# Weight slots of 1024 columns at set distances from the activations, and the first stage's K tiles in two units

## The chip, the cores and the metric

The kernel runs on one core of one Trainium2 chip. The metric is the device time of one execution in microseconds. The kernel before takes 1234.42 us, the median of three runs (1234.06 to 1234.61).

## What is computed

One layer of a hybrid decoder for 256 tokens and a model width of 2048, in float32. Cut to its products:

```
h    = rmsnorm(x) ; proj = h @ w_in          # pool group | q | k | v | indexer q, k, weights
pool = trailing means minus token, per-group linear map, scale
attn = attention of 8 heads over the 64 keys per query that the indexer picks, with a T5 bias
x   += concat(pool, attn) @ w_out
u    = rmsnorm(x) @ w_up                     # 2048 x 11264
uc   = causal depthwise conv of width 3 of u
x   += (silu(gate) * val) @ w_down           # 5632 x 2048
x   += (p @ w_ple_proj) * sigmoid(rmsnorm(x) @ w_ple_gate)
out  = rmsnorm(x)
```

## The kernel before, in words

Every weight passes through SBUF once, in units. `unit` (lines 59 to 68) loads n columns with a DMA on SP's queue into a tile `raw`, has ScalarE (ACT) copy them to `hi` in the type float32r, which drops low bits, and VectorE (DVE) write `lo = raw - hi`, so that hi + lo is exact. There are four slots for raw, three for hi and three for lo; each slot is UNIT = 1104 columns wide, which is what the first stage needs (one K tile of 128 rows of v, indexer keys and head weights is 1104 columns). Slots are taken in turn, and a slot is taken again when what reads it is done. All other stages load units of 1024 columns. The activations are kept as hi and lo parts side by side, 256 columns each.

The products come in two forms. In `cm_matmul` (line 121) the weights are stationary: for each of the eight K tiles of a unit, TensorE (PE) loads a 128x128 tile of hi and streams hT's 512 columns (activations' hi and lo), then loads the tile of lo and streams 256 columns. `cm_tile` (line 130) makes one column tile of 128 outputs of two units: 32 such tiles in the mixer (indexer queries, q and k, the pool group), 88 in the up-projection. In `tm_matmul` (line 143) the activations are stationary and 512 columns of the unit are streamed, three times for each K tile and half of the tokens: 12 matmuls a unit. So are the first stage (368 columns, 16 K tiles, lines 210 to 230), the output projection (32 units, activations `catP` and `catA`), the down-projection (88 units, `aT`) and the gate (32 units, `hT`; the last 8 are kept in tiles of their own).

A load of the next stationary tile goes on while the matmul before it streams. Each engine runs its instructions in order. The order is made by a planner when the program is built, from its own model of times; `keep_in_program_order` pins some of the DMAs. SP's queue carries nearly all loads. ACT's queue carries a few: among them the table of relative biases is written to DRAM (`bd`, line 326) and read back shifted (`tb`, line 328), and the second waits for the first.

Tiles are laid out in SBUF one pool behind the other, in the order in which the pools are opened. In the built program of before a partition holds, by byte address: hT 36064; raw 74240, 78656, 83072, 87488; hi 91904, 96320, 100736; lo 105152, 109568, 113984; then small buffers, catP 125952, and in the later stages aT 132096. The three pairs of hi and lo slots are called A, B and C in the order of their addresses. A tile of hT has 2048 bytes, a K tile of a unit 512 bytes where the weights are stationary and 2048 where they stream. Modulo 512, hi and lo lie this far beyond hT: A 32 and 480, B 352 and 288, C 160 and 96; aT lies beyond hi and lo: A 256 and 320, B 448 and 0, C 128 and 192.

Of the kernel before, what the change touches and what calls it, by code (L numbers as in the profile page):

```python
# [10 lines left out]
F32 = mybir.dt.float32  # L11
# [7 lines left out]
P = 128  # L19
# [9 lines left out]
TOPK = 64  # L29
# [4 lines left out]
NVK = (NH * P + 80) // 3  # L34
UNIT = 3 * NVK

# columns of the packed per-channel parameters
C_GMIX, C_GFFN, C_GPLE, C_PS, C_CONV = 0, 16, 32, 48, 56
# columns of the packed constants
K_ACC0, K_ACC1, K_PEN0, K_PEN1, K_OH, K_INV = 0, 128, 384, 512, 768, 1152  # L40
# [4 lines left out]
def layer(ctx: ExitStack, tc: tile.TileContext, a: dict):  # L45
    nc = tc.nc
    in_order = tc.keep_in_program_order
    V, A, T, G = nc.vector, nc.scalar, nc.tensor, nc.gpsimd

    cst = ctx.enter_context(tc.tile_pool(name="cst", bufs=1))  # L50
    wraw = ctx.enter_context(tc.tile_pool(name="wraw", bufs=4))
    whi = ctx.enter_context(tc.tile_pool(name="whi", bufs=3))
    wlo = ctx.enter_context(tc.tile_pool(name="wlo", bufs=3))
    tmp = ctx.enter_context(tc.tile_pool(name="tmp", bufs=2))
# [4 lines left out]
    def unit(src, n=1024, keep=None):  # L59
        """n weight columns on chip as the exact sum hi + lo of two float32r parts"""  # L60
        size, bufs = (1024, 8) if keep else (UNIT, None)
        raw = wraw.tile([P, UNIT], F32, name="raw")
        nc.sync.dma_start(raw[:, :n], src)
        hi = (keep or whi).tile([P, size], F32R, name="hi", bufs=bufs)
        A.copy(hi[:, :n], raw[:, :n])  # L65
        lo = (keep or wlo).tile([P, size], F32R, name="lo", bufs=bufs)
        V.tensor_sub(lo[:, :n], raw[:, :n], hi[:, :n].bitcast(F32))  # L67
        return hi, lo

# [1 line left out]
    prm = cst.tile([P, C_CONV + S], F32, name="prm")  # L71
# [49 lines left out]
    def cm_matmul(ps, hi, lo, kts, first, last):  # L121
        """weights stationary: ps[:, :256] + ps[:, 256:] = w.T @ hT"""
        for i, kt in enumerate(kts):
            w = slice(i * P, (i + 1) * P)
            T.matmul(ps, hi[:, w], hT[:, kt, :], start=first and i == 0, stop=False)  # L125
            T.matmul(ps[:, :S], lo[:, w], hT[:, kt, :S],  # L126
                     start=False, stop=last and i == len(kts) - 1)
# [15 lines left out]
    def tm_matmul(pss, hi, lo, act, kts, first, last, toks=(0, 1), n=512, w0=0):  # L143
        """activations stationary: pss[t] = act[:, tok t].T @ w"""
        for i, kt in enumerate(kts):
            w = slice(w0 + i * n, w0 + (i + 1) * n)
            for t in toks:
                xh = act[:, kt, t * P:(t + 1) * P]
                xl = act[:, kt, S + t * P:S + (t + 1) * P]
                T.matmul(pss[t][:, :n], xh, hi[:, w], start=first and i == 0, stop=False)  # L150
                T.matmul(pss[t][:, :n], xh, lo[:, w], start=False, stop=False)  # L151
                T.matmul(pss[t][:, :n], xl, hi[:, w], start=False,  # L152
                         stop=last and i == len(kts) - 1)

    def to_hT(n, gcol):
        """columns n*512.. of the residual stream, transposed, times g, split"""
        for kp in range(2):
            ps = aux.tile([P, 512], F32, name="ps")
            for j in range(2):
                kt = 4 * n + 2 * kp + j  # L160
                for t in range(2):
                    T.transpose(ps[:, j * S + t * P:j * S + (t + 1) * P],  # L162
                                x[:, t, kt * P:(kt + 1) * P], ident)
            for j in range(2):
                kt = 4 * n + 2 * kp + j
                split(hT[:, kt, :S], hT[:, kt, S:], ps[:, j * S:(j + 1) * S],
                      prm[:, gcol + kt:gcol + kt + 1])
# [15 lines left out]

    # =====================================================================
    with ExitStack() as c1:
        ar = c1.enter_context(tc.tile_pool(name="ar", bufs=1))
        catP = ar.tile([P, 8, 2 * S], F32R, name="catP")

# [1 line left out]
        xr = [ar.tile([P, 8, S], F32, name="xr0", tag="tb"),  # L190
# [10 lines left out]

        # the tensor engine's clock rises while the first loads are under way
        warm = aux.tile([P, 512], F32, name="ps")
# [4 lines left out]
        for kt in range(KT):  # L208
            if kt == 1 or (kt and kt % 2 == 0):
                k1 = kt + 1 if kt == 1 else kt + 2  # L210
                nc.sync.dma_start(xr[kt // 8][:, kt % 8:(k1 - 1) % 8 + 1, :],
                                  a["xT"][:, kt:k1, :])
            cuts = (0, NVK, 3 * NVK) if kt == 0 else (0, 3 * NVK)
            ws = [unit(a["w_first"][kt][:, c0:c1], c1 - c0) for c0, c1 in zip(cuts, cuts[1:])]
            split(hT[:, kt, :S], hT[:, kt, S:],
                  xr[kt // 8][:, kt % 8, :] if kt else prm[:, C_CONV:],
                  prm[:, C_GMIX + kt:C_GMIX + kt + 1])
            for n in range(3):
                i = sum(n * NVK >= c for c in cuts) - 1
                tm_matmul(pvk[n], *ws[i], hT, (kt,), kt == 0, kt == KT - 1, n=NVK,  # L220
                          w0=n * NVK - cuts[i])
            if kt == 3:
                in_order(nc.sync.dma_start(ident, a["ident"]))
            if kt in (5, 7, 9, 11):
                c = (kt - 5) // 2
                cs = slice(c * 512, (c + 1) * 512)
                in_order(nc.sync.dma_start(x[:, :, cs], a["x"][:, :, cs]))
            if kt in (9, 11, 13, 15):
                square_x((kt - 9) // 2)
# [5 lines left out]

# [1 line left out]
        kd = ar.tile([P, 2, 2, 64], F32, name="kd")  # L237
# [25 lines left out]

# [1 line left out]
        s0 = [cc[:, K_ACC0:K_ACC0 + P], cc[:, K_ACC1:K_ACC1 + S]]  # L265
        sc = [ar.tile([P, P], F32, name="sc0"), ar.tile([P, S], F32, name="sc1")]

        def query(ps):
            """fp32 for the first 128 tokens; for the others the rows of a head are followed
            by (or follow) their low parts, so that one product over 128 rows takes both"""  # L270
            qx = ar.tile([P, S], F32, name="qx", bufs=3)
# [47 lines left out]

# [1 line left out]
        psb = aux.tile([P, 512], F32, name="ps")  # L321
# [8 lines left out]

# [1 line left out]
        one = ar.tile([P, S], F32, name="one")  # L332
# [29 lines left out]

# [1 line left out]
        L = [ar.tile([P, NH, P], F32, name="L0"), ar.tile([P, NH, S], F32, name="L1", tag="L1")]  # L364
# [67 lines left out]

# [1 line left out]
        plr = None  # L434
# [56 lines left out]

# [1 line left out]
        def out_units(n, pss, gs, first, last):  # L493
# [17 lines left out]

    # =====================================================================
    pin = ctx.enter_context(tc.tile_pool(name="pin", bufs=1))
# [4 lines left out]
    with ExitStack() as c2:  # L518
        far = c2.enter_context(tc.tile_pool(name="far", bufs=1))
        aT = far.tile([P, NF, 2 * S], F32R, name="aT")  # L520
        r_ffn = rstd_col(sum4(ssq_f), "r_ffn")
# [22 lines left out]

        # the first two tiles leave the last K tiles to the end: those come from the last
        # columns of the residual stream
        ps2 = [acc.tile([P, 512], F32, name="pa") for _ in range(2)]
# [7 lines left out]

# [1 line left out]
        for n in range(4):  # L557
# [6 lines left out]

    # =====================================================================
    with ExitStack() as c3:
# [27 lines left out]
        def store(t, slots):  # L594
            """the last slot joins the sum of those before it"""
            ms = gar.tile([P, 1], F32, name=f"ms{t}")
# [44 lines left out]
def _cm(w):  # L641
    """(K, C) -> (C/128, 128, K/128*128): rows of a partition for one column tile together"""
    k, c = w.shape
    return np.ascontiguousarray(
        w.reshape(k // P, P, c // P, P).transpose(2, 1, 0, 3).reshape(c // P, P, k))


def _tm(w, n=512):
    """(K, N) -> (N/512, 128, K/128*512)"""
    k, c = w.shape  # L650
    return np.ascontiguousarray(
        w.reshape(k // P, P, c // n, n).transpose(2, 1, 0, 3).reshape(c // n, P, k // P * n))
# [72 lines left out]
```

## Time and profile before

| | |
|---|---|
| median of the runs | 1234.42 us |
| span of the profiled execution | 1232.6 us; the runs lie 1.5 to 2.0 us above it |
| PE busy | 1199.4 us, 97% of the span, 6332 matmuls |
| PE weight loads busy | 1027.0 us, 83% |
| DVE, ACT busy | 816.1 us (66%), 625.5 us (51%) |
| PE, up-projection's hi and lo matmuls with the mixer's | 1904 of each |
| DMA | 230.44 MB, mean 187 GB/s; 352 GB/s in the first of 40 slices |
| granted clock | 0.989 of 2.4 GHz, mean over the span |

PE's busy time counts each matmul from its start to a modelled end, and matmuls overlap, so the sum of durations is more than the time they take. The distance between the starts of two matmuls in a row is what one costs. Times in the timeline are us from the span's start.

### The profile page before, as it was taken

How to read it: one execution, taken by the hardware profiler on the slowest of the kernel's cores; microseconds unless marked ns; L12 is line 12 of the kernel's file. 1: busy time of each engine (PE TensorE's matmuls, PEld its weight loads, DVE VectorE, ACT ScalarE, POOL GpSimd, SP SyncE). 2: the span in 40 equal slices, each digit the busy share in tenths (PEclk: the TensorE clock that was granted, in tenths of full speed). 3: DMA queues.
4: the chain of work that ended last, by engine and by line, in shares of the span. 5: the costliest groups of instructions: out<-in, count | busy, mean ns of one | idle time of the engine just before them, and what ended most of it. 6: DMA issues, size and time to landing. Idle time of an engine off the chain costs nothing.

```text
span 1232.6 us, 16720 instructions
## 1 busy us (share of the span) xinstructions
PE 1199.4 (97%) x6332; PEld 1027.0 (83%) x6332; DVE 816.1 (66%) x1234; ACT 625.5 (51%) x951; POOL 5.5 (0%) x23
## 2 busy tenths in 40 slices
PE   9999669999999999999999999999999999999996
PEld 8988558888888888888888888888888888888886
DVE  6566465796555877787777877788645454545565
ACT  7455134565454655555555555555434343434453
POOL 0000000000000000000000000000000000000000
PEclk9999879999999999999999999999999999999998
DMA  9654555545655655555555565566666666666662
GB/s 352 222 185 146 126 171 191 161 148 178 188 173 168 210 190 189 189 188 189 189 189 190 189 190 190 191 189 192 189 188 185 190 182 191 181 194 213 188 217 87
DMA packets 67784, 230.44 MB, mean 187 GB/s; under 512 B 7416, under 2 KB 11128, under 8 KB 67576
## 3 DMA queue, kind: packets, MB, share of 16 engines
q1 hardware_dynamic: 63488, 223.88, 57.8%
q10 hardware_dynamic: 4216, 5.51, 2.1%
q8 instruction: 49, 0.80, 0.3%
q14 instruction: 31, 0.25, 0.1%
HBM read 225.16 MB, written 3.67 MB: 186 GB/s over the span
## 4 chain that ended last, share of the span: by engine, by line
PE 95%; DMA 3%; ACT 1%; DVE 0%; SPq 0%; issue 0%; POOLq 0%; ACTq 0%
PE pa L125 35%; PE pa L126 18%; PE pa L151 12%; PE pa L152 12%; PE pa L150 12%; DMA bd<-bv 3%; PE ps L151 1%; PE ps L152 1%; PE ps L150 1%; PE ps L162 1%; DMA raw<-in_w_first 0%; PE ps L465 0%; PE ps L290 0%; ACT hi L65 0%; PE ps L375 0%; PE ps L291 0%
## 5 line engine op out<-in xcount | busy, mean ns | idle before, releaser
L67 DVE TENSOR_TENSOR lo<-raw,hi 128x1024 fp32r<-128x1024 f32 (+2 forms) x417 | 508.5, 1220 | 373.5 <-ACT hi L65 370.6
L65 ACT CAST hi<-raw 128x1024 fp32r<-128x1024 f32 (+2 forms) x417 | 435.8, 1046 | 555.3 <-issue 218.7
L125 PE MATMUL pa<-hT,hi 128*128 128x512 f32 x1904 | 667.8, 394 | 20.3 <-ACT hi L65 20.3
L126 PE MATMUL pa<-hT,lo 128*128 128x256 f32 x1904 | 534.5, 281 | 0.5 <-DVE lo L67 0.5
L125 PEld LDWEIGHTS pa<-hT,hi 128*128 128x128 f32 x1904 | 358.4, 188 | 102.4 <-ACT hi L65 21.0
L126 PEld LDWEIGHTS pa<-hT,lo 128*128 128x128 f32 x1904 | 358.6, 188 | 1.2 <-DVE lo L67 1.0
L152 PE MATMUL pa<-hi,aT 128*128 128x512 f32 x352 | 138.4, 393 | 0.0
L151 PE MATMUL pa<-lo,aT 128*128 128x512 f32 x352 | 138.3, 393 | 0.0
L150 PE MATMUL pa<-hi,aT 128*128 128x512 f32 x352 | 125.9, 395 | 0.0
L151 PEld LDWEIGHTS pa<-lo,aT 128*128 128x128 f32 x352 | 66.0, 188 | 15.6
L152 PEld LDWEIGHTS pa<-hi,aT 128*128 128x128 f32 x352 | 66.0, 188 | 15.1
L150 PEld LDWEIGHTS pa<-hi,aT 128*128 128x128 f32 x352 | 66.1, 188 | 15.0
L151 PE MATMUL pa<-lo,hT 128*128 128x512 f32 (+2 forms) x208 | 74.4, 358 | 0.1
L152 PE MATMUL pa<-hi,hT 128*128 128x512 f32 (+2 forms) x208 | 74.3, 358 | 0.0
L150 PE MATMUL pa<-hi,hT 128*128 128x512 f32 (+2 forms) x208 | 64.4, 359 | 1.4 <-ACT hi L65 1.4
L532 ACT ACTIVATE cv<-ub,cnv 128x256 f32<-128x256 f32 x88 | 52.6, 598 | 1.0 <-DVE ub L141 1.0
L140 DVE TENSOR_TENSOR eb<-pa,eb 128x256 f32<-128x256 f32 x119 | 49.6, 417 | 0.0
L536 DVE SCALAR_TENSOR_TENSOR cv<-ub,cnv,cv 128x256 f32<-128x256 f32 x88 | 42.6, 485 | 3.0
L150 PEld LDWEIGHTS pa<-hi,hT 128*128 128x128 f32 x208 | 38.3, 188 | 7.2 <-ACT hi L65 2.0
L151 PEld LDWEIGHTS pa<-lo,hT 128*128 128x128 f32 x208 | 39.1, 188 | 5.7 <-DVE lo L67 0.7
L139 ACT COPY eb<-pa 128x256 f32<-128x256 f32 x119 | 43.5, 365 | 0.0
L152 PEld LDWEIGHTS pa<-hi,hT 128*128 128x128 f32 x208 | 39.1, 188 | 5.0
(171 smaller groups left out, 822.2 us busy)
## 6 DMA issues: line engine op xcount, KB each, us to landing
raw<-in_w_up SPq DMA_DIRECT2D x176, 512.0 KB, 3.8
raw<-in_w_down SPq DMA_DIRECT2D x88, 512.0 KB, 3.6
raw<-in_w_qk SPq DMA_DIRECT2D x32, 512.0 KB, 3.9
raw<-in_w_out SPq DMA_DIRECT2D x32, 512.0 KB, 3.7
raw<-in_w_pg SPq DMA_DIRECT2D x32, 512.0 KB, 3.9
raw<-in_w_first SPq DMA_DIRECT2D x15, 552.0 KB, 6.4
raw<-in_w_qi SPq DMA_DIRECT2D x16, 512.0 KB, 4.6
raw<-in_w_u SPq DMA_DIRECT2D x16, 512.0 KB, 3.7
```

What stands on the lines that cost most here:

```text
L65: A.copy(hi[:, :n], raw[:, :n])
L67: V.tensor_sub(lo[:, :n], raw[:, :n], hi[:, :n].bitcast(F32))
L125: T.matmul(ps, hi[:, w], hT[:, kt, :], start=first and i == 0, stop=False)
L126: T.matmul(ps[:, :S], lo[:, w], hT[:, kt, :S], start=False, stop=last and i == len(kts) - 1)
L139: A.copy(b, ps[:, S:])
L140: V.tensor_add(b, ps[:, :S], b)
L150: T.matmul(pss[t][:, :n], xh, hi[:, w], start=first and i == 0, stop=False)
L151: T.matmul(pss[t][:, :n], xh, lo[:, w], start=False, stop=False)
L152: T.matmul(pss[t][:, :n], xl, hi[:, w], start=False, stop=last and i == len(kts) - 1)
L162: T.transpose(ps[:, j * S + t * P:j * S + (t + 1) * P], x[:, t, kt * P:(kt + 1) * P], ident)
L532: A.activation(t, u[:, 2:], AF.Identity, bias=cnv[:, k + 3:k + 4], scale=cnv[:, k + 2:k + 3])
L536: V.scalar_tensor_tensor(t, u[:, :S], cnv[:, k:k + 1], t, op0=OP.mult, op1=OP.add)
```

## The change

UNIT becomes 1024, so every slot has 4096 bytes, and the slots of one part (raw, hi or lo) have the same address modulo 1024. Pools with one tile each that nothing reads or writes are opened between raw and hi (16 columns of 4 bytes) and between hi and lo (240 columns), and one of 80 columns stands ahead of aT. A K tile of the first stage no longer fits a slot and is loaded, split and multiplied in two units of 736 and 368 columns (K tile 0 was two units of 368 and 736 before, and stays so). Comments are dropped from the file. The diff without them:

```
-UNIT = 3 * NVK
+UNIT = 1024
...
     wraw = ctx.enter_context(tc.tile_pool(name="wraw", bufs=4))
+    gap0 = ctx.enter_context(tc.tile_pool(name="gap0", bufs=1))
     whi = ctx.enter_context(tc.tile_pool(name="whi", bufs=3))
+    gap1 = ctx.enter_context(tc.tile_pool(name="gap1", bufs=1))
     wlo = ctx.enter_context(tc.tile_pool(name="wlo", bufs=3))
...
+    def place(pool, n):
+        pool.tile([P, n], F32, name="place")
+
+    place(gap0, 16)
+    place(gap1, 240)
...
-            cuts = (0, NVK, 3 * NVK) if kt == 0 else (0, 3 * NVK)
+            cuts = (0, NVK, 3 * NVK) if kt == 0 else (0, 2 * NVK, 3 * NVK)
...
         far = c2.enter_context(tc.tile_pool(name="far", bufs=1))
+        place(far, 80)
         aT = far.tile([P, NF, 2 * S], F32R, name="aT")
```

## Rows read from the trace of the kernel before

**Rows 1.** Busy time of each engine in stretches: from:to in us, length, then busy us and instructions of PE, weight loads, DVE, ACT, POOL, the granted clock, DMA share and GB/s.

```profile
8.50:13.30 4.80, 4.39 (x24) 3.78 (x24) 3.55 (x5) 4.40 (x6) 0.00 (x0) 1.00 1.03 404
13.30:49.50 36.20, 36.20 (x217) 36.20 (x216) 22.11 (x30) 22.93 (x40) 0.70 (x1) 1.00 0.89 325
...
400.00:888.00 488.00, 488.00 (x2789) 427.50 (x2788) 388.16 (x616) 280.04 (x438) 0.00 (x0) 1.00 0.60 191
888.00:1136.00 248.00, 248.00 (x1090) 201.40 (x1089) 119.89 (x117) 103.59 (x120) 0.69 (x1) 1.00 0.65 191
```

**Rows 2.** The page's chain of the work that ended last: shares of the span by engine, then by line.

```profile
PE 95%; DMA 3%; ACT 1%; DVE 0%; SPq 0%; issue 0%; POOLq 0%; ACTq 0%
PE pa L125 35%; PE pa L126 18%; PE pa L151 12%; PE pa L152 12%; PE pa L150 12%; DMA bd<-bv 3%; PE ps L151 1%; PE ps L152 1%; PE ps L150 1%; PE ps L162 1%; DMA raw<-in_w_first 0%; PE ps L465 0%; PE ps L290 0%; ACT hi L65 0%; PE ps L375 0%; PE ps L291 0%
```

**Rows 3.** PE's timeline in the up-projection: start in us, length in us, engine, line, tiles. The first matmul of four units in a row, in the slots B, A, C, B.

```profile
704.61 0.39 PE L125 MATMUL pa<-hT,hi 128*128 128x512 f32 x1
...
707.36 0.39 PE L125 MATMUL pa<-hT,hi 128*128 128x512 f32 x1
...
710.14 0.40 PE L125 MATMUL pa<-hT,hi 128*128 128x512 f32 x1
...
712.96 0.39 PE L125 MATMUL pa<-hT,hi 128*128 128x512 f32 x1
```

**Rows 4.** The same view early in the up-projection: hi matmuls of a unit in slot B that begins at 404.06 us, and the start of the next unit, 406.87.

```profile
404.06 0.39 PE L125 MATMUL pa<-hT,hi 128*128 128x512 f32 x1
...
404.40 0.40 PE L125 MATMUL pa<-hT,hi 128*128 128x512 f32 x1
...
404.75 0.40 PE L125 MATMUL pa<-hT,hi 128*128 128x512 f32 x1
...
405.82 0.39 PE L125 MATMUL pa<-hT,hi 128*128 128x512 f32 x1
...
406.16 0.40 PE L125 MATMUL pa<-hT,hi 128*128 128x512 f32 x1
...
406.87 0.39 PE L125 MATMUL pa<-hT,hi 128*128 128x512 f32 x1
```

**Rows 5.** The same view in the mixer, units in slot B that come first behind other work on PE: hi matmuls that are five pairs apart, in the units that begin at 95.96, 228.67 and 254.68 us.

```profile
95.96 0.39 PE L125 MATMUL pa<-hT,hi 128*128 128x512 f32 x1
...
97.73 0.39 PE L125 MATMUL pa<-hT,hi 128*128 128x512 f32 x1
...
229.82 0.39 PE L125 MATMUL pa<-hT,hi 128*128 128x512 f32 x1
...
231.58 0.39 PE L125 MATMUL pa<-hT,hi 128*128 128x512 f32 x1
...
255.93 0.39 PE L125 MATMUL pa<-hT,hi 128*128 128x512 f32 x1
...
257.69 0.39 PE L125 MATMUL pa<-hT,hi 128*128 128x512 f32 x1
```

**Rows 6.** The same view where the up-projection begins.

```profile
397.93 0.39 PE L125 MATMUL pa<-hT,hi 128*128 128x512 f32 x1
398.57 0.51 PE L125 MATMUL pa<-hT,hi 128*128 128x512 f32 x1 [0.25 <-ACT hi L65]
```

**Rows 7.** The same view in the down-projection: the first two matmuls of four units in a row, in the slots A, C, B, A.

```profile
950.07 0.63 PE L150 MATMUL pa<-hi,aT 128*128 128x512 f32 x2
...
952.85 0.62 PE L150 MATMUL pa<-hi,aT 128*128 128x512 f32 x2
...
955.60 0.63 PE L150 MATMUL pa<-hi,aT 128*128 128x512 f32 x2
...
958.40 0.63 PE L150 MATMUL pa<-hi,aT 128*128 128x512 f32 x2
```

**Rows 8.** Groups of ACT's instructions by line and shape in the first stage, 3 to 55 us: count, busy us, mean ns of one, idle us before them and what ended it.

```profile
L65 ACT CAST hi<-raw 128x1104 fp32r<-128x1104 f32 x15 | 16.7, 1116 | 12.6 <-PE ps L152 10.3 <-DMA raw<-in_w_first 1.9 <-DVE hT L94 0.2
...
L65 ACT CAST hi<-raw 128x736 fp32r<-128x736 f32 x1 | 0.8, 804 | 1.8 <-DMA raw<-in_w_first 1.8
...
L65 ACT CAST hi<-raw 128x368 fp32r<-128x368 f32 x1 | 0.5, 498 | 0.0
```

**Rows 9.** The same for DVE.

```profile
L67 DVE TENSOR_TENSOR lo<-raw,hi 128x1104 fp32r<-128x1104 f32 x15 | 19.6, 1307 | 14.4 <-ACT hi L65 14.2
...
L67 DVE TENSOR_TENSOR lo<-raw,hi 128x736 fp32r<-128x736 f32 x1 | 0.9, 926 | 2.1 <-ACT hi L65 2.1
...
L67 DVE TENSOR_TENSOR lo<-raw,hi 128x368 fp32r<-128x368 f32 x1 | 0.5, 542 | 0.0
```

**Rows 10.** DMA issues: count, KB each, median us from issue to landing.

```profile
raw<-in_w_first SPq DMA_DIRECT2D x15, 552.0 KB, 6.4
...
raw<-in_w_first SPq DMA_DIRECT2D x1, 368.0 KB, 4.2
```

**Rows 11.** Waits: who waited for whom, us in total, times, longest us.

```profile
ACT hi L65 <- DMA bd<-bv: 26.6, 1, 26.6
```

## The prediction

> **What bounds the kernel now.** I read the stretches first: in 400 to 888 us (up-projection) and 888 to 1136 us (down-projection) PE is busy for the whole stretch at the full 2.4 GHz level, with DVE at 388 of 488 us and ACT at 280 [rows 1]. The chain of waits says the same: PE is 95% of it, one DMA (bd) is 3% [rows 2]. So a change counts by what it does to the distance between the starts of two matmuls. The busy time of a matmul doesn't show that, as matmuls overlap; I read starts.
>
> **What the starts say of addresses.** A unit of the weights-stationary part is eight pairs: a 512-column matmul with hi, a 256-column one with lo. Streamed without any loss, a pair is 768 columns at 2.4 GHz, 320 ns. In the up-projection the three slots take turns, B, A, C, and their units last 707.36 - 704.61 = 2.75 us (B), 710.14 - 707.36 = 2.78 (A) and 712.96 - 710.14 = 2.82 (C) [rows 3]. Same work, same clock, other addresses: 344, 348 and 353 ns a pair. While a matmul streams, the load of the next stationary tile reads too, and the slots differ in the distance between the two. In the down-projection the order is another one: A 2.78, C 2.75, B 2.80 us [rows 7]. One K tile further is 512 bytes further in the slot, so a distance modulo 1024 takes two values in turn. But a rhythm that repeats after five pairs, an odd number, is seen too (404.06 and 405.82 us both begin a pair of 0.34, the next ones take 0.35 [rows 4]); so the two values act alike, and I take distances modulo 512.
>
> Modulo 512, slot B has hi 352 and lo 288 beyond hT, and slot C has aT 128 beyond hi and 192 beyond lo. From the new sizes: hT stays at 36064, raw ends at 74240 + 4 x 4096 = 90624, hi begins 64 bytes on at 90688, lo at 90688 + 3 x 4096 + 960 = 103936, and all behind it moves down 2176 bytes, aT up again by 320, to 130240. Distances: hi 54624, lo 67872 beyond hT, which is 352 and 288; aT is 39552 beyond hi and 26304 beyond lo, which is 128 and 192. So every up-projection unit becomes a B and every down-projection unit a C, each the shortest in its stage.
>
> **The choice: B has two rhythms.** The 2.75 us of B isn't the address alone. At 404.06 us a B unit lasts 2.81 us, its hi matmuls mostly 0.35 us apart, five pairs in 405.82 - 404.06 = 1.76 us, which is 352 ns a pair [rows 4]. It comes again whenever a B unit is the first behind other work on PE: 1.77 us at 95.96 (behind the indexer's matmuls), 1.76 us at 229.82 and at 255.93 (last five pairs of units behind the logits' matmuls) [rows 5]. I found no B unit that changes from one rhythm to the other on its way. In the long stretch of the up-projection B has the short rhythm, but there it always follows a C unit. The changed kernel has no C units before B units: every unit is a B, and the stage begins behind a stop (two hi starts 0.64 us apart at 397.93 [rows 6]). What decides is the rhythm in which such a stage starts and stays. All starts that I see behind other work are in the long one, so I take 8 x 0.352 = 2.816 us a unit.
>
> **The sum.** Up-projection: 88 column tiles of two units, 176. Before, a mean of (2.75 + 2.78 + 2.82) / 3 = 2.783 us; after, 2.816: +0.033 x 176 = +5.8 us. Mixer (indexer, q, k, pooling): 32 tiles, 64 units. A and C cost what they cost above, B there is in part at 2.75, in part at 2.81, a mean of about 2.79; after, 2.816 again: +0.026 x 64 = 1.7, and I take +1.5, as a few units lie beside the stop on bd. Down-projection: 88 units, before (2.78 + 2.75 + 2.80) / 3 = 2.777, after C alone, 2.755 with the digit that the rows round off: -0.02 x 88 = -1.8 us. There I see no second rhythm that lasts.
>
> Output projection (32 units) and gate (24 units in slots, 8 in tiles of their own): catP, catA and hT are now the loaded operand at distances of which only hT's has been seen with these slots (it is slot B's). By the nearest rows, units of twelve matmuls at 2.75 to 2.80 us [rows 7], the two stages lie within 1.4 us either way of a unit in the middle; I take 0. Casts and subtractions keep their sizes after the first stage.
>
> First stage. Each K tile now has two DMAs, two casts and two subtractions: 0.80 + 0.50 against 1.12 us on ACT, 0.93 + 0.54 against 1.31 on DVE [rows 8, 9], so +0.18 and +0.16 for each of 15 K tiles, beside PE, whose K tile is 18 matmuls of 36.2 / 217 = 0.167 us, 3.0 us [rows 1]. That is hidden, but the cover is thinner: four raw slots held four K tiles and now hold two, three hi slots held three and now one and a half. SP's queue issues in order, so what stands behind a unit's DMA that waits for its slot (the next xT, x, ident) waits too. A raw slot serves every second K tile, so within 6.0 us it must be loaded (368 KB), cast (0.80) and subtracted (0.93): it holds while a landing takes less than 4.3 us. The one 368 KB load of before took 4.2, the 552 KB loads 6.4, with twice as much under way [rows 10]. For it speaks the start: 0.41 us of the stretch from 8.50 to 13.30 us is idle PE [rows 1], and a first unit that is a third smaller lands and is cast sooner. I take 0, from -0.7 to, at the worst, the +15 us of a rival below.
>
> The stop on bd: ACT stands 26.6 us at a cast until bd has landed [rows 11], as the DMA that reads bd back waits in ACT's order. The change doesn't touch it, but the order is the planner's, and one cast more or less ahead of that DMA is one unit, 2.8 us, either way. I take the same order.
>
> Sum: +5.8 + 1.5 - 1.8 = +5.5 us. The profiled execution has a span of 1232.6 us, 1.8 under the median of the runs (1234.4): 1238.1 us of span, **1239.9 us**. Its own range is 1237 to 1244, from the two stages (1.4 each), the planner's unit (2.8) and 3 us for the first stage.
>
> **Rivals.** *The short rhythm holds*: if the up-projection falls into B's 2.75 us at its start, nothing in it would disturb it either. Then 176 x (2.75 - 2.783) = -5.8, in the mixer, where matmuls of other kinds come between, about -1, and -1.8: 1225.8 us, clearly faster. For it: 2.75 is what B shows in most units of rows 3's stage, and behind C both a short-rhythm and a long-rhythm unit were followed by a short one. Against it: no start without a C unit. It decides by the first pairs behind 398 us. 20%.
>
> *Addresses do nothing*: the differences between slots would come from what ACT and DVE do at the time; then only the first stage moves and it is 1234 to 1236 us. Against it, the order of slots turns round between the stages [rows 3, 7]. The Trainium skill (SBUF — State Buffer, Who interferes with whom) holds that the moving operand and the weight load have a read port each, and that PE never waits on anyone; by that rule this rival is the forecast, and the trace doesn't agree: 2.75 against 2.82 us for the same eight pairs. 7%.
>
> *The first stage starves*: if landings stay at 6.4 us, the cycle of a raw slot is 6.4 + 0.80 + 0.93 = 8.1 us for two K tiles in place of 6.0: +2.1 x 7 = +15 us, 1255 us with the rest. Against it: half as much is under way. 6%.
>
> *The placeholders take no room* (a tile that nothing writes or reads): hi would be 288 beyond hT as lo is, a pair of distances that no slot has; anything between all units at 2.75 and all at 2.82, 1226 to 1241 us. 5%.
>
> **How the numbers follow.** The forecast has 62%. Its time is the prediction. The range of 1225 to 1244 takes in the short rhythm and leaves out the starving stage and the far ends. Less than 0.2%, 2.5 us, counts as no change. Faster: the short rhythm's 20% and 4% of the placeholders and lucky orders. Same: 12%, the second rival and the forecast's lower tail with a planner's unit won. Slower: 64%.
>
> **What would show it.** In the changed kernel's starts of hi matmuls between 400 and 890 us: all units alike is the address step; 2.81 to 2.82 us is the forecast, 2.75 the first rival, three lengths in turn the second. Down-projection units of 2.75 to 2.76 us confirm its step. An idle PE between 13 and 55 us is the first stage's cover gone. The ACT cast ahead of the stop on bd tells the planner's order. The prediction falls if units of slot-B distances that begin behind other work run at 2.75 us.

## The result and the profile after

The changed kernel takes 1247.15 us, the median of four runs, beside 1234.51 us of before in the same measurement: a ratio of 1.0106, 95% interval 1.0081 to 1.0131. It is slower, and 7 us more so than forecast. No run took 1247 us: two took 1253.3 and 1253.5, two 1240.6 and 1241.0. The profiled execution is one of the long ones, 1253.53 us with a span of 1251.7, 19.1 us more than before's. Why there are two times is one of the questions below.

PE's timeline, read at the first matmul of each stage in both kernels, says where the 19.1 us are:

| stage, first matmul to the next stage's | before, us | after, us | change | forecast |
|---|---|---|---|---|
| first stage (from 1.13 us) | 54.81 | 67.26 | +12.45 | 0 |
| mixer up to bd's matmul | 69.26 | 70.58 | +1.33 | +1.5 with the next row |
| mixer behind it | 162.87 | 163.67 | +0.80 | |
| output projection | 94.50 | 94.23 | -0.27 | 0 |
| up-projection | 491.72 | 497.38 | +5.66 | +5.8 |
| down-projection | 246.90 | 246.06 | -0.84 | -1.8 |
| gate to the end | 111.44 | 111.39 | -0.05 | 0 |

All stages but the first sum to +6.6 us where +5.5 was forecast. The first stage, taken at nothing, lost 12.45.

The first stage in stretches, with the columns of [rows 1], and two shorter stretches of the second line:

```profile
8.50:13.30 4.80, 4.80 (x30) 4.80 (x29) 4.80 (x11) 4.66 (x12) 0.00 (x0) 1.00 1.03 379
13.30:49.50 36.20, 30.16 (x152) 28.04 (x151) 15.29 (x25) 16.36 (x35) 0.00 (x0) 0.91 0.64 198
...
28.80:32.20 3.40, 3.40 (x13) 3.40 (x12) 1.70 (x3) 0.81 (x1) 0.00 (x0) 0.50 0.84 197
45.90:49.30 3.40, 3.40 (x13) 3.40 (x12) 1.74 (x3) 0.81 (x1) 0.00 (x0) 0.50 0.75 186
```

The stage starts well: 30 matmuls in the first stretch where before had 24, the gain from the smaller first units that the forecast allowed. Then 152 matmuls come in 36.2 us where 217 came. PE idles 6.0 us of it, and the matmuls that do run take 30.16 / 152 = 0.198 us each and not 0.167: 4.8 us more for 152, and 10.8 us lost in this stretch. Most of the 4.8 is the clock: in the two shorter stretches, behind stops of PE of 3.6 and 2.2 us, the granted clock is 0.50, the 1.2 GHz level, and some 22 matmuls start 0.307 us apart and not 0.168, 3.1 us in all. The rest lies mainly in the first matmuls behind each stop, 0.26 to 0.31 us apart at a granted clock of 1.00. The DMA share fell from 0.89 to 0.64, so the stage isn't short of bandwidth: something holds the loads back.

The waits, 8.5 to 62 us (who waited for whom, us in total, times, longest):

```profile
DVE lo L69 <- ACT hi L67: 21.6, 14, 6.0
ACT sq L208 <- DMA x<-in_x: 18.7, 4, 5.2
PEld ps L159 <- ACT hi L67: 8.1, 4, 3.9
PE ps L159 <- ACT hi L67: 6.9, 4, 3.6
```

Read from the bottom: PE waits for casts, and ACT, which makes them, stands 18.7 us at four squares of x. `square_x` is no part of the product; its sums are needed at the stage's end. But ACT runs in order, and the casts stand behind it. The same wait before, with the squares at nearly the same place in ACT's order (there behind the cast of every second K tile, here between that K tile's two casts):

```profile
ACT sq L199 <- DMA x<-in_x: 0.2, 1, 0.2
```

So x is late. Issues on SP's queue in the changed kernel (start, length, line, tiles; a length over several DMAs includes what SP waited), and then three of the four squares of ACT that wait (in brackets the idle time ahead of one):

```profile
17.39 0.66 SPq L236 DMA_DIRECT2D x<-in_x  x1
18.61 9.77 SPq L65 DMA_DIRECT2D raw<-in_w_first  x4
28.43 0.55 SPq L236 DMA_DIRECT2D x<-in_x  x1
29.14 7.63 SPq L65 DMA_DIRECT2D raw<-in_w_first  x4
36.83 0.55 SPq L236 DMA_DIRECT2D x<-in_x  x1
```

```profile
25.73 0.63 ACT L208 ACTIVATE sq<-x 128x512 f32<-128x512 f32 x1 [5.17 <-DMA x<-in_x]
...
34.12 0.63 ACT L208 ACTIVATE sq<-x 128x512 f32<-128x512 f32 x1 [4.20 <-DMA x<-in_x]
...
42.88 0.63 ACT L208 ACTIVATE sq<-x 128x512 f32<-128x512 f32 x1 [4.63 <-DMA x<-in_x]
```

This is a loop that holds itself: ACT at a square waits for x; behind it wait the casts, and for those the subtractions; only a subtraction frees a raw slot; SP needs four raw slots before it reaches the next x; and the next square waits for that x. A turn is a square at 25.73, the next x issued at 28.43 (2.70 us), landed 5.67 us later, the next square at 34.12: 8.39 us, then 8.76. PE needs 6.0 for those two K tiles. Before, the four raw slots let SP run four K tiles ahead, and the second x was issued 13 us earlier:

```profile
12.74 0.65 SPq L227 DMA_DIRECT2D x<-in_x  x1
13.50 1.68 SPq L63 DMA_DIRECT2D raw<-in_w_first  x2
15.46 0.55 SPq L227 DMA_DIRECT2D x<-in_x  x1
```

The up-projection, the first matmul of three units in a row and of the fourth, as in [rows 3]:

```profile
640.82 0.39 PE L134 MATMUL pa<-hT,hi 128*128 128x512 f32 x1
...
643.63 0.40 PE L134 MATMUL pa<-hT,hi 128*128 128x512 f32 x1
...
646.44 0.40 PE L134 MATMUL pa<-hT,hi 128*128 128x512 f32 x1
...
649.26 0.40 PE L134 MATMUL pa<-hT,hi 128*128 128x512 f32 x1
```

2.81, 2.81 and 2.82 us: all units alike, in the long rhythm. The down-projection, as in [rows 7]:

```profile
978.14 0.62 PE L159 MATMUL pa<-hi,aT 128*128 128x512 f32 x2
...
980.91 0.63 PE L159 MATMUL pa<-hi,aT 128*128 128x512 f32 x2
...
983.67 0.62 PE L159 MATMUL pa<-hi,aT 128*128 128x512 f32 x2
```

2.77 and 2.76 us, a mean of 2.767 over the stage, not the 2.755 that a C unit took before between others. The wait on bd is 26.6 us as in [rows 11]: that order is the same.

### The profile page after: what moved, and what is told of

The parts are those of the page before. It is cut to its first block, busy times and chain, and to the rows that moved or that the text cites. A ratio compares the mean times of both kernels' runs of the same rounds, so it can differ in the third digit from the quotient of the medians.

```text
span 1251.7 us, 16809 instructions
## 1 busy us (share of the span) xinstructions
PE 1210.7 (97%) x6332; PEld 1032.6 (82%) x6332; DVE 818.1 (65%) x1249; ACT 626.1 (50%) x966; POOL 5.7 (0%) x23
## 4 chain that ended last, share of the span: by engine, by line
PE 90%; DMA 6%; DVE 1%; ACT 1%; issue 1%; SPq 0%; POOLq 0%; ACTq 0%; DVEq 0%
PE pa L134 35%; PE pa L135 18%; PE pa L159 11%; PE pa L160 11%; PE pa L161 11%; DMA bd<-bv 3%; DMA x<-in_x 2%; ACT hi L67 1%; DVE lo L69 1%; PE ps L171 1%; DMA raw<-in_w_qi 1%; PE ps L474 0%; PE ps L299 0%; PE ps L384 0%; DVE hT L103 0%
## 5 line engine op out<-in xcount | busy, mean ns | idle before, releaser
L69 DVE TENSOR_TENSOR lo<-raw,hi 128x1024 fp32r<-128x1024 f32 (+3 forms) x432 | 510.7, 1184 | 390.8 <-ACT hi L67 390.0
L67 ACT CAST hi<-raw 128x1024 fp32r<-128x1024 f32 (+3 forms) x432 | 437.0, 1015 | 557.8 <-issue 221.2
```

## The experiments

### The first stage

**two_units**: the kernel before with the new cuts alone, slots and addresses as they were.

```
-            cuts = (0, NVK, 3 * NVK) if kt == 0 else (0, 3 * NVK)
+            cuts = (0, NVK, 3 * NVK) if kt == 0 else (0, 2 * NVK, 3 * NVK)
```

> Only the cut of the first stage's K tiles into two units (0..736..1104) on the kernel before; slots of 1104 columns and all addresses stay. Theory 1 (ACT's squares wait for x, whose DMA stands on SP's queue behind weight DMAs that wait for a raw slot): 1234 us or up to +12.5 us above, 1247 us, with squares of x waiting 4 to 5 us each, and units of the up-projection at 2.75, 2.78, 2.82 us as before. Rival (the new slot size or addresses make the first stage slow): the first stage ends at 56 us and the time is 1234 to 1235 us in every run.

1248.66 us (1247.16 to 1249.97), ratio 1.0119, interval 1.0104 to 1.0134. The first stage takes 67.95 us, 13.1 more than before; the up-projection takes 491.70 us as before. The same wait is there:

```profile
ACT sq L199 <- DMA x<-in_x: 17.9, 4, 4.8
```

So the cut alone makes the loss, and addresses have no part in it.

**late** and **late3**: the changed kernel with the squares moved back in ACT's order, by four K tiles and by three. (The expectation of late3 says two K tiles earlier than late and two behind the changed kernel. In the traces the first squares stand behind a cast of K tile 5 in the changed kernel, 8 in late3 and 9 in late, counted from 0.) All DMAs stay in their order on SP.

```
+            if kt in (8, 10, 12, 14):
+                square_x((kt - 8) // 2)
             split(hT[:, kt, :S], hT[:, kt, S:],
...
-            if kt in (9, 11, 13, 15):
-                square_x((kt - 9) // 2)
```

(This is late3; late has 9, 11, 13 and 15 there. In both the squares are pinned in program order.)

> The changed kernel with the squares of x four K tiles later in ACT's order; all DMAs in their order. Theory 1 (the squares' wait for x holds back the casts behind it): the loss of the first stage goes, 1240 to 1241 us in every run, no wait of ACT for x over 1 us, first stage 55 to 57 us. Rival (the landings alone starve the stage: with four raw slots for two K tiles a slot's load, cast and subtraction take more than the 6.06 us that PE needs for two K tiles): PE's idle time before the casts stays, 1250 to 1254 us. Third (the rhythm of the up-projection makes the two times): they appear here too.

> The changed kernel with the squares of x two K tiles earlier in ACT's order than in the run with the late squares, still two K tiles behind their place in the changed kernel. Theory 1 (ACT's wait for x made the first stage's loss; the late squares only moved 4.4 us of it to the stage's end, where PE waited for r_mix): first stage ends at 56 to 59 us, no wait of ACT for x over 1.5 us and none of PE for r_mix over 1 us; 1242 to 1244 us in the long rhythm of the up-projection, 1230 to 1232 in the short one. Rival (weight landings set the pace whatever ACT's order): first stage ends at 61 us or later, with ACT waiting for raw in place of x.

late gave 1235.31 us in the profiled execution and 1247.65 to 1248.73 in six others (median 1248.14, ratio 1.0102, 1.0073 to 1.0131), not the 1240 to 1241 expected; its first stage took 60.46 us. ACT no longer waits for x, but 4.1 us of the gain was lost again at the end of the stage, because the last sum was now late:

```profile
PE ps L126 <- DVE r_mix L120: 4.1, 1, 4.1
```

late3 settles it: 1242.31 us (1240.86 to 1243.27), ratio 1.0066 (1.0050 to 1.0083). Its first stage takes 55.56 us, 0.75 more than before. No wait for x and none for r_mix is left; what ACT now waits for is raw, 10.1 us in six times, and PE hardly feels it:

```profile
13.30:49.50 36.20, 35.63 (x208) 34.58 (x207) 19.32 (x31) 20.50 (x43) 0.00 (x0) 1.00 0.80 254
```

The same cut, the same slots, the same order of loads, and the loss is gone: it was the place of eight small instructions in ACT's order. The landing time of the 368 KB loads, from issue to landing, falls with it, from a median of 5.9 us (8.5 to 62 us) in the changed kernel to 4.4.

### The two times and the rhythm

**after_again**: the changed kernel once more.

> The changed kernel as it is, to see where its two times (1240.6 and 1253.5 us) part. Theory 1, the first stage: the profile that took 1251.7 us of span has its first stage 12.45 us longer than before, with ACT at the squares of x waiting 4 to 5 us for x in each two K tiles; in a run of about 1241 us the first stage ends near 56 us after the span's start and the up-projection's units last 2.81 to 2.82 us all the same. Rival, the rhythm: the up-projection's units last 2.75 us in the shorter runs (176 x 0.066 = 11.6 us) and the first stage loses its 12 us in all of them.

Only the long time came: 1251.98 us (1251.48 to 1252.53), ratio 1.0146 (1.0131 to 1.0161), first stage 66.42 us, up-projection 497.44. That told nothing of the short time. The profiled execution of late did: it is 13 us under the other six, and its up-projection took 485.67 us. Its first six units take 2.81 us or more, and all from 411.6 us on take 2.75:

```profile
656.04 0.39 PE L134 MATMUL pa<-hT,hi 128*128 128x512 f32 x1
...
658.79 0.39 PE L134 MATMUL pa<-hT,hi 128*128 128x512 f32 x1
...
661.54 0.39 PE L134 MATMUL pa<-hT,hi 128*128 128x512 f32 x1
```

Same addresses, same instructions, 2.747 us a unit and not 2.816. So slots at B's distances have two rhythms, and a long run of B units keeps the one in which it starts: 176 x 0.069 = 12 us. Where the choice falls can be seen in the changed kernel (the line with x2 holds two 256-column matmuls in a row):

```profile
413.36 0.39 PE L134 MATMUL pa<-hT,hi 128*128 128x512 f32 x1
...
415.08 0.39 PE L134 MATMUL pa<-hT,hi 128*128 128x512 f32 x1
...
415.65 0.40 PE L135 MATMUL pa<-hT,lo 128*128 128x256 f32 x2
...
416.24 0.40 PE L134 MATMUL pa<-hT,hi 128*128 128x512 f32 x1
...
418.00 0.40 PE L134 MATMUL pa<-hT,hi 128*128 128x512 f32 x1
```

Behind a stop of 0.25 us, five pairs take 1.72 us, the short rhythm. Then two 256-column matmuls come in a row, and from there five pairs take 1.76 us, the long rhythm to the end. In late the same place turns it the other way: five pairs take 1.76 us from 406.59 and 1.72 from 410.22. What each stop or break of the alternation does to the rhythm was not tried by itself.

**bbc** puts B units behind C units: two slots at B's distances, the third at C's.

```
-    place(gap0, 16)
-    place(gap1, 240)
+    place(gap0, 16)
+    place(gaph, 80)
+    place(gap1, 32)
+    place(gapl, 80)
```

(The three slots of a part become pools of one tile; gaph and gapl stand ahead of the third. In the last stages aT moves with them.)

> The changed kernel with two of the three slots at B's distances beyond hT (hi 352, lo 288 modulo 512) and the third at C's (160 and 96). Theory 1 (a B unit is short, 2.75 us, only if a C unit runs ahead of it): the B unit behind C lasts 2.75 us; the second B, behind a B, keeps that rhythm, since all-B units kept theirs: 2.82, 2.75, 2.75, a mean of 2.773 against 2.816, 7.5 us less in the up-projection, +1.4 us in the down-projection: 6 us under the changed kernel. Theory 2 (the second B falls back into the long rhythm): 2.82, 2.75, 2.81, a mean of 2.793, 4 us less. Rival (slots of 1024 columns have the long rhythm whatever runs ahead): 2.82 us throughout, no difference.

```profile
658.55 0.40 PE L140 MATMUL pa<-hT,hi 128*128 128x512 f32 x1
...
661.37 0.39 PE L140 MATMUL pa<-hT,hi 128*128 128x512 f32 x1
...
664.12 0.39 PE L140 MATMUL pa<-hT,hi 128*128 128x512 f32 x1
...
666.87 0.40 PE L140 MATMUL pa<-hT,hi 128*128 128x512 f32 x1
```

A C unit from 658.55 to 661.37, 2.82 us, then two B units of 2.75. The up-projection took 490.29 us, 7.1 under the changed kernel; the first expectation holds there. The 1.4 us more that it gave the down-projection did not come (245.96 us), and the whole, 1250.03 us (1247.89 to 1250.79), ratio 1.0125 (1.0108 to 1.0142), is only 2 under the changed kernel: the mixer behind bd took 168.34 us, 4.7 more. With pools of one tile the planner put a half-width cast of the pool group and several others elsewhere; b_plain below tells that this is the cause.

**addr_only**: the address part without the cut. The first stage keeps units of 1104 columns in memory that is free at that time, all else lies at the changed kernel's distances.

```
+        fw = [ar.tile([P, 8, 2 * S], F32R, name=f"fw{j}", tag=t).rearrange("p a b -> p (a b)")
+              for j, t in enumerate(("catP", "qkA"))]
...
+        if first:
+            hi, lo = (f[:, k * UNIT:(k + 1) * UNIT] for f in first)
```

> The address part alone. The first stage keeps one unit of 1104 columns a K tile, four raw slots of 1104, and its hi and lo parts lie in memory that catP and catA use later; all other units lie in slots at B's distances from hT and C's from aT, as in the changed kernel. Theory (the parts add up): first stage as before, ending near 56 us; up-projection +5.7, mixer +1.9, down-projection -0.8 us: 1240 to 1241 us where the up-projection runs in the long rhythm (2.81 to 2.82 us a unit), 1228 to 1229 us where it falls into the short one (2.747 us a unit). Rival (the up-projection is slow because of what the first stage leaves behind, or of smaller raw slots): units at 2.75 us in every run, about 1229 us.

1242.68 us (1240.53 to 1245.05), ratio 1.0067 (1.0052 to 1.0083). First stage 54.13 us, 0.7 less than before; up-projection 497.38, down-projection 246.06, to 0.01 us what the changed kernel has. The parts add up, but for the mixer behind bd, 167.19 us: pools of one tile again, and the same other order as in bbc. PE idles 2.4 us here between 260 and 275 us, where it had no idle time before:

```profile
260.00:275.00 15.00, 12.62 (x82) 10.92 (x81) 11.78 (x22) 9.17 (x19) 0.49 (x4) 1.00 0.43 133
```

**kick**: addr_only with the third slot's unit shifted to C's distances in every eighth pair of column tiles.

```
+            shift[0] = 80 if KICK and c % 8 == 1 else 0
```

> The kernel of addr_only, but in the up-projection the third slot's unit is shifted by 80 columns, to C's distances, in every eighth pair of column tiles (22 of 176 units or fewer). Theory (a B unit takes the short rhythm when a C unit runs ahead of it, and keeps it behind another B): 2.747 us for nearly all units from the first C on, 484 to 486 us for the up-projection in every run, 1228 to 1230 us, faster than before by 4 to 6 us. Rival (the short rhythm behind C is lost again after one or two units): as addr_only in its long rhythm, 1240 us.

1236.4 us (1233.74 to 1237.92), ratio 1.0015 (1.0005 to 1.0024); up-projection 490.58 us. The expectation fell in part: the whole stayed 6 us above the 1228 to 1230 forecast, because the mixer behind bd took 169.52 us and the rhythm turned late. One C unit alone, at 496.32 us, left the rhythm long. Two with two B units between them turned it:

```profile
580.81 0.39 PE L140 MATMUL pa<-hT,hi 128*128 128x512 f32 x1
...
583.64 0.39 PE L140 MATMUL pa<-hT,hi 128*128 128x512 f32 x1
...
586.45 0.40 PE L140 MATMUL pa<-hT,hi 128*128 128x512 f32 x1
...
589.27 0.40 PE L140 MATMUL pa<-hT,hi 128*128 128x512 f32 x1
...
592.09 0.40 PE L140 MATMUL pa<-hT,hi 128*128 128x512 f32 x1
...
594.85 0.39 PE L140 MATMUL pa<-hT,hi 128*128 128x512 f32 x1
```

C 2.83, B 2.81, B 2.82, C 2.82, then B 2.76 and from there 2.747 to the end, past further single C units. In bbc the turn came at the same place, behind the second C unit of its stretch at 433.90 us.

**after_kick**: the changed kernel with its stalling first stage, and in the second to seventh pair of column tiles every third unit in the still empty end of aT, at C's distances.

```
+            tail[:] = [aT.rearrange("p c s -> p (c s)")[:, o:o + 1024]
+                       for o in (36 * 512 + 48, 40 * 512 + 32)] if c <= 6 else []
...
+        if tail and turn[0] % 3 == 0:
+            hi, lo = tail
```

> The changed kernel, first stage and all, with one difference: in the second to seventh pair of column tiles of the up-projection every third unit lies in the still empty end of aT, at C's distances. Theory (the changed kernel's two times are the two rhythms of its up-projection, and its first stage loses 12 us in both): first stage ends at 67 to 69 us, up-projection 485 to 487 us, 1240 to 1241 us in every run, as its two shorter runs had. Rival (the first stage makes the two times): both times again, 1240 and 1252 us.

1241.05 us (1240.25 to 1242.91, five runs), ratio 1.0053 (1.0039 to 1.0067). First stage 66.82 us, up-projection 485.83. The long time didn't come; with the rhythm held short, the changed kernel has its shorter time with the stall in it. That its own runs of 1240.6 and 1241.0 us were such executions is read from their times; neither was profiled.

### Which distances are slow, and a kernel that is faster than both

**sweep**: addr_only with wider slots, each unit shifted inside its slot, in steps of 64 bytes.

> The kernel of addr_only with slots of 1152 columns, each unit shifted inside its slot: in the up-projection hi and lo together by 0, 64, ... 448 bytes (ten units each), then lo alone by 256 and by 128 more (six units each); in the down-projection by 0 to 448 bytes, 11 units each. Three intermediate buffers of the mixer and gate have one slot less. Theory (the distance modulo 512 sets the pitch): the shift of 192 gives A's 2.78 us, that of 320 C's 2.82, that of 0 B's 2.75 or 2.81; others between 2.74 and 2.83. Rival (only the order of slots matters): all shifts alike.

One run, 1242.28 us. Each shift ran for twenty units of the up-projection (the expectation says ten), and of lo's own shifts only the first came in. Hi's and lo's distance beyond hT, modulo 512, and the steady unit:

| hi, lo beyond hT | unit, us |
|---|---|
| 32, 480 (A) | 2.773 |
| 96, 32 | 2.816 |
| 160, 96 (C) | 2.827 |
| 224, 160 | 2.773 |
| 288, 224 | 2.773 |
| 352, 288 (B, long) | 2.816 |
| 416, 352 | 2.827 |
| 480, 416 | 2.827 |
| 352, 32 | 2.816 |

Two units of the third row from below and two of A's, by their starts:

```profile
470.37 0.40 PE L142 MATMUL pa<-hT,hi 128*128 128x512 f32 x1
...
473.20 0.40 PE L142 MATMUL pa<-hT,hi 128*128 128x512 f32 x1
...
599.80 0.39 PE L142 MATMUL pa<-hT,hi 128*128 128x512 f32 x1
...
602.57 0.39 PE L142 MATMUL pa<-hT,hi 128*128 128x512 f32 x1
```

Three lengths, with B's short rhythm a fourth, and B's long one is that of 96, 32 too. The shifts of 192 and 320 bytes gave A's and C's lengths, as expected. The last row differs from B in lo alone and has B's length: there lo's place made no difference. In the down-projection aT at 64 and 128 beyond hi and lo gave 2.753 us, less than C's 2.767.

**b_plain**, **b_kick** and **all_a** take this up. b_plain is addr_only with the slots of a part back in one pool of three and aT at 64 and 128 beyond; b_kick adds the eight C units of after_kick; all_a has A's distances in all slots.

```
-KICK, G0, FAR = 0, 80, 64
+KICK, G0, FAR = 6, 80, 64
```

(b_kick against b_plain; all_a has 0, 0, 64: no columns in the pool ahead of hi.)

> The kernel of addr_only, with its hi and lo slots back in two pools of three that take turns (so the mixer's casts keep the order that they had before) and aT 64 and 128 beyond hi and lo. All up-projection units at B's distances. Theory (addr_only lost 4.3 us in the mixer by the planner's order, not by addresses): from bd's matmul to the output projection 163 to 164 us, up-projection 497.4, down-projection 245 (2.753 us a unit, read from the sweep): 1236 to 1237 us in the long rhythm, 1224 to 1226 in the short one. Rival (addresses cost the mixer 4 us): 1240 to 1241.

> The kernel of b_plain, but in the second to seventh pair of column tiles of the up-projection every third unit lies in the still empty end of aT, at C's distances (160 and 96). Theory (two C units with two B units between them turn the rhythm to the short one, as in bbc and in kick at 587 us, and it then stays): 2.747 us for nearly all units from about 420 us on, up-projection 485 to 487 us, 1224 to 1227 us in every run, 0.993 of before. Rival (whether a C unit turns the rhythm is chance): times from 1225 to 1237 us.

> The kernel of b_plain with all slots at A's distances from hT (32 and 480), aT as there. Theory (A has one rhythm, 2.773 us, read from the sweep): up-projection 489 to 490 us, 1228 to 1230 us in every run, all within 2 us. Rival (A too has a slower rhythm that the sweep didn't meet): 2.80 us or more, 1234 us or above.

| | us | ratio | interval | mixer behind bd | up | down |
|---|---|---|---|---|---|---|
| b_plain | 1224.89 (1223.79 to 1237.37, 10 runs) | 0.9934 | 0.9915 to 0.9954 | 162.03 | 485.68 | 244.91 |
| b_kick | 1225.76 (1225.04 to 1226.18, 5 runs) | 0.9927 | 0.9914 to 0.9939 | 163.03 | 485.84 | 244.90 |
| all_a | 1231.56 (1230.37 to 1232.56, 8 runs) | 0.9972 | 0.9962 to 0.9982 | 163.18 | 490.00 | 247.25 |

b_kick is the version to keep: faster than before by 0.7% in every run. By its times b_plain fell into the short rhythm in nine of ten runs and into the long one in the tenth, 1237.37 us. With one pool of three the mixer is about as before: addr_only's 4.3 us were the order. all_a holds one rhythm as expected, but it stays 2 us above the 1228 to 1230 forecast, because its down-projection is slower: with aT at the same 64 and 128 beyond hi and lo as in b_plain, its units take 2.78 us where b_plain's take 2.75:

```profile
956.24 0.63 PE L168 MATMUL pa<-hi,aT 128*128 128x512 f32 x2
...
959.02 0.63 PE L168 MATMUL pa<-hi,aT 128*128 128x512 f32 x2
```

```profile
949.71 0.62 PE L168 MATMUL pa<-hi,aT 128*128 128x512 f32 x2
...
952.47 0.62 PE L168 MATMUL pa<-hi,aT 128*128 128x512 f32 x2
```

Both kernels' aT is 38976 bytes beyond the first hi slot; all_a's lie 320 bytes lower. So the distance modulo 512 is not the whole of it. Whether the places themselves count, or this form too has two rhythms, wasn't tried.

## Why the prediction was right and wrong

**First stage: wrong, and the step that failed.** "I take 0", it says, because a raw slot "must be loaded (368 KB), cast (0.80) and subtracted (0.93): it holds while a landing takes less than 4.3 us". That budget was about right: late3, with landings of 4.4 us, loses 0.75 us. What failed is that the budget takes ACT to be at hand for the cast. The step itself says that "what stands behind a unit's DMA that waits for its slot (the next xT, x, ident) waits too", and stops at the queue. It had to go on to who reads x and what stands behind that reader: `square_x`, ahead of the casts in ACT's order. Half the depth in K tiles alone moves the second x from 15.46 to 22.84 us (late3); with the squares in their old place the loop moves it to 28.43. The price is 12.45 us, shown by two_units (the cut alone, +13.1) and late3 (the squares alone moved, -11.7). Before's trace showed the thin margin: the squares waited 0.2 us, once.

**The rival of the starving stage** came close in its price, +15 us, for another reason. It had landings at 6.4 us as the cause. They took 5.9, but with the squares moved the same loads in the same order land in 4.4: the slow landings went with the stall and did not make it.

The Trainium skill (Perfetto Trace Analysis, Optimization Strategy) reads a gap that repeats on the engine that should be full as a sign that there may be too few or too small buffers for the next tile. Here the gap repeats four times, and fewer K tiles in the slots did open it; but late3 closes it with the same slots, so the sign leads to the place and not to the only cure.

**Up-projection: right for the profiled execution, with luck.** "+0.033 x 176 = +5.8 us"; measured 497.38 - 491.72 = +5.66, with units of 2.81 to 2.82 us. That B has two rhythms and that a long run of B units keeps one was the right reading [rows 4, 5]. That starts behind other work are in the long one is no rule: the changed kernel's own trace has short pairs behind the stop at 412.91 us, and late and b_plain ran short. By the prediction's own sign ("units of slot-B distances that begin behind other work run at 2.75 us") this step fell in those two.

**The rival of the short rhythm** is no other outcome of one kernel but the other state of the same one: by their times, two of the eight runs of the changed kernel fell into it, as did one of seven of late. The prediction gave it 20% and its price, 5.8 us under before in this stage: late has 485.67, 6.05 under. What it missed is that both happen, so that a median of few runs lies anywhere between.

The Trainium skill (SBUF — State Buffer, Who interferes with whom) gives the moving operand and the weight load a read port each and has PE wait for no one. If nothing else counted, addresses would make no difference, and the traces don't agree: 2.747, 2.773, 2.816 and 2.827 us for the same eight pairs. What PE loses the time to, they don't show.

**Mixer: near in size, but only in part for its reason.** +1.5 forecast, +2.1 measured (1.33 + 0.80). Ahead of bd, 1.4 us are idle PE at the mixer's first unit, which waits for its cast and its subtraction behind the late first stage:

```profile
68.39 0.50 PE L134 MATMUL ps<-hT,hi 128*128 128x512 f32 x1 [0.66 <-ACT hi L67]
69.65 0.39 PE L135 MATMUL ps<-hT,lo 128*128 128x256 f32 x1 [0.76 <-DVE lo L69]
```

two_units, with the addresses of before, idles 1.9 us there and takes 2.57 more in this stretch; b_kick, with B's distances and no such stop, takes 0.15 more. Behind bd the +0.80 fits the long rhythm: 336 pairs start 351.5 ns apart in the mean where before has 349.2.

**Down-projection: mechanism right, size off.** "C alone, 2.755", so -1.8 us; measured 2.767 and -0.84. The term took a C unit's 2.755 us from a sequence in which it always follows an A unit. Behind its own kind it takes 0.01 us more, 88 times, in all three slots, and in the sweep at other places too. So the unit ahead most likely makes the difference, which is the mistake that the prediction avoided for B.

**The stop on bd, the output projection and the gate** moved by 0, -0.27 and -0.05 us against 0. The placeholders take room: units are of one length, as calculated for these addresses. **Addresses do nothing** is refuted by all runs.

The forecast's own range, 1237 to 1244, had 3 us for the first stage. The other stages took 1.1 us more than their terms (6.6 against 5.5), so by this sum without the first stage's loss the changed kernel would be at 1241.0 us in the long rhythm; late3, which is nearly that kernel, measures 1242.31.

## What to carry to other kernels

When a buffer's depth is halved, follow each DMA that shares the issuing queue to the instruction that reads it, and look what stands behind that instruction on its engine: a side computation ahead of casts in an in-order engine can turn a late load into a loop that feeds itself. Where matmuls and weight loads stream without a wait, measure the distance between starts by slot, and behind which neighbour; a unit's length in a mixed sequence doesn't say what a sequence of its own kind takes. And when the runs of one kernel fall into two groups, profile both before the median is explained.

## What was not expected of the hardware

- The same sequence of matmuls and weight loads at the same addresses has two stable rhythms, 2.747 and 2.816 us for a unit. Each lasted for all of the 169 units behind an up-projection's start, over 460 us. One C unit among long B units turned nothing; two with two units between them turned long to short, in bbc and in kick. Short to long came behind two 256-column matmuls in a row, at 415.65 us in the changed kernel.
- At A's distances and at C's only one rhythm showed in the up-projection, and the sweep found nothing under 2.773 us.
- Equal distances at other absolute addresses gave 2.753 and 2.780 us in the down-projection. What sets this stays open.
- PE's idle time cost more than itself: in the first stage, 6.0 us of idle PE came with 4.8 us more in the matmuls that ran, 3.1 of it at a granted clock of 0.50. Not every stop was followed by such a stretch: in two_units PE stopped for 2.7 us up to 27.4 us, and the granted clock fell to 0.50 only at 36.1 us, behind a second stop of 2.1 us.
